# A decoder step on one core: norm sums by one product with ones, prompt rows transposed by VectorE, small work in larger groups

## The chip, the cores and the metric

The kernel runs on one core of a Trainium2 chip. The metric is device time in microseconds (us) of one execution; lower is better. Names of engines in the profile: PE is TensorE (PEld its weight loads), DVE is VectorE, ACT is ScalarE, POOL is GpSimd, SP is the queue that issues most transfers.

## The reference

One layer of a hybrid decoder for 256 prompt tokens and 32 sample tokens (8 sequences of 4), with a model width of 2048, all in float32. Cut to what matters here:

```python
def rms_norm(x, g):
    y = x * lax.rsqrt(jnp.mean(x * x, axis=-1, keepdims=True) + RMS_EPS)
    return y * g

def decoder_layer(x, mk, mv, conv_past, pool_past, pos0, ...):
    h = rms_norm(x, g_mix)
    z = h @ w_in                                   # 2048 -> 11264 columns
    u, v, c, p, gate = jnp.split(z, SPLITS, axis=-1)
    y_a, v_state = chunk_mixer(u, v, ...)          # u * (tril(W_s) LN(v) + b_s), 4 heads
    y_b, conv_state = conv_module(c, conv_past, ...)   # GLU, 31-tap conv, LayerNorm, swish
    y_c, pool_state = pool_mixer(p, pool_past, ...)    # trailing means, linear map
    br = jnp.einsum('bsnc,ncd->bsnd', jnp.stack([y_a, y_b, y_c], axis=2), w_branch)
    merged = jnp.sum(jax.nn.sigmoid(gate) * br, axis=2)
    x = x + merged @ w_out
    x = x + cross_attn(rms_norm(x, g_xattn), mk, mv, w_xq, w_xo)
    hm = rms_norm(x, g_mlp)
    x = x + jnp.square(jax.nn.relu(hm @ w_up)) @ w_down
    return x, v_state, conv_state, pool_state
```

The outputs are the normed x of both groups, the new memory keys and values, and states: the last 30 GLU rows and the last 15 pooling rows of each sequence (new_conv_p and new_pool_p for the prompt), and the normed v rows.

## The kernel before

**Layout.** Activations stand transposed: 128 channels on the partitions, 288 token columns (256 prompt, 32 sample) in the free dimension. A product of 2048 inputs and 512 outputs (proj) runs over 16 k-tiles into four PSUM accumulators of 128x288; there are eight PSUM buffers in all. To keep float32 precision, each operand is split in a high and a low part (w_hi, w_lo; q_hi, q_lo), and every product is three matmuls (L239 to L241).

**Weights.** A chunk of 512x512 (1 MB) is loaded by the SP queue into one of three raw buffers. It is used in two halves of two k-tiles, 24 matmuls each. For each half ScalarE writes w_hi (L172) and VectorE writes w_lo = raw - w_hi (L173). There are three buffers of each, and next_half(i) calls advance(i), which splits half i + 2 (AHEAD = 2); so a half's split is issued two halves before its products.

**Order of other work.** After each half tick() runs. It moves a clock on by one and runs every piece of work that later(n, fn) has put down n steps before, and a few taps of the convolution from a background list. The order of instructions on every engine is the order in which the Python code issues them; each engine executes its own in that order.

**Statistics.** The squares of x (or of the centred convolution) are summed over the 8 or 16 channel tiles into one accumulator of 128x288, acc (square_acc, L334). Still to be summed are the 128 partitions. stats_later does it in three steps, each one tick apart: token_rstd multiplies acc with a column of ones, so that the tokens come to stand on the partitions (L288), scales (L290, L291) and takes the power -0.5 on GpSimd over 128x2 and 32x1 elements (rpow, L283); token_diag makes a diagonal matrix of the result (L300); broadcast_tokens multiplies it with a matrix of ones (L306), which spreads each token's factor over all partitions, and copies it to rb (L308). It is called three times: for the convolution's LayerNorm (used by conv_out, L775, five ticks later), and at the end of residual for the norm before cross attention (used in evac_q, L944) and before the MLP (used in evac_up, L1144). In the last two the factor is used at the first evacuation, since a row's scale can be applied behind the product.

**Prompt states.** rows_out transposes four channel tiles at a time on TensorE (L573), copies them on ScalarE (L574) and issues a transfer from ScalarE's queue; two quarters for the convolution (L589) and two for the pool (L601).

**Others that the change touches.** state_transposed (L457) turns the incoming states, four transposes (L461) and four VectorE copies (L463) at a time, six times. mixing (L705) computes one channel tile of branch A: three products and three VectorE operations, eight times, one tick apart. rows_keep (L1184) transposes four finished channel tiles for the output, nine times.

Of the kernel before, what the change touches and what calls it, by code (L numbers as in the profile page):

```python
# [8 lines left out]
F32 = mybir.dt.float32  # L9
F32R = mybir.dt.float32r  # L10
AF = mybir.ActivationFunctionType
ALU = mybir.AluOpType
# [4 lines left out]
P = 128  # L17
# [4 lines left out]
NT = NP + NS  # L22
# [4 lines left out]
PP = 15  # L27
# [4 lines left out]
TOK = ((0, 128), (128, 128), (256, 32))  # L32
# [6 lines left out]
def decoder_step_kernel(  # L39
# [10 lines left out]
    v_, s_, g_, t_ = nc.vector, nc.scalar, nc.gpsimd, nc.tensor  # L50
# [8 lines left out]
    small = ctx.enter_context(tc.tile_pool(name="small", bufs=2))  # L59
# [7 lines left out]
    def psum():  # L67
        t = ps_pool.tile([P, 512], F32, name="ps", tag="ps")
        return t
# [3 lines left out]
    ones = const.tile([P, P], F32, name="ones")  # L73
    v_.memset(ones, 1.0)
    mhalf = const.tile([P, 3], F32, name="mhalf")
# [21 lines left out]
    def later(n, fn):  # L97
        clock[1] += 1
        pending.append((clock[0] + n, clock[1], fn))
# [143 lines left out]
    def proj(w, nkt, n0, act, evac, bg=0, w_k0=0, last=False):  # L243
        acc = [psum() for _ in range(4)]
        for kc in range(0, nkt, 4):
            if last and kc == nkt - 4:
                hl = [next_half(w, w_k0 + kc + 2 * half, n0) for half in range(2)]
                for j in range(4):
                    for i in range(4):
                        product(acc, act, *hl[i // 2], kc + i, i % 2, j, nkt)  # L250
                    evac(j, acc[j][:, :NT])
                tick()
                return
            for half in range(2):
                hi, lo = next_half(w, w_k0 + kc + 2 * half, n0)
                for i in range(2):
                    kt = kc + 2 * half + i
                    for j in range(4):
                        product(acc, act, hi, lo, kt, i, j, nkt)
                tick(bg)  # L260
        for j in range(4):
            evac(j, acc[j][:, :NT])
# [19 lines left out]
    def rpow(out, ms):  # L282
        g_.tensor_tensor(out, ms, mhalf[:ms.shape[0], :ms.shape[1]], ALU.pow)  # L283

    def token_rstd(acc, n, eps):
        st = psum()
        for i, (t0, tn) in enumerate(TOK):
            t_.matmul(st[:tn, i:i + 1], acc[:, t0:t0 + tn], ones[:, 0:1], start=True, stop=True)  # L288
        ms = small.tile([P, 3], F32, name="ms")
        v_.tensor_scalar(ms[:, 0:2], st[:, 0:2], 1.0 / n, eps, ALU.mult, ALU.add)  # L290
        v_.tensor_scalar(ms[:32, 2:3], st[:32, 2:3], 1.0 / n, eps, ALU.mult, ALU.add)  # L291
        r = small.tile([P, 3], F32, name="r_tok")
        rpow(r[:, 0:2], ms[:, 0:2])
        rpow(r[:32, 2:3], ms[:32, 2:3])
        return r

    def token_diag(r):
        dg = small.tile([P, NT], F32, name="dg", tag="t288", bufs=4)
        for i, (t0, tn) in enumerate(TOK):
            v_.tensor_scalar(dg[:tn, t0:t0 + tn], ident[:tn, :tn], r[:tn, i:i + 1], None, ALU.mult)  # L300
        return dg

    def broadcast_tokens(dg):
        out = psum()
        for t0, tn in TOK:
            t_.matmul(out[:, t0:t0 + tn], ones[:tn, :], dg[:tn, t0:t0 + tn], start=True, stop=True)  # L306
        rb = small.tile([P, NT], F32, name="rb")
        v_.tensor_copy(rb, out[:, :NT])  # L308
        return rb

    def stats_later(acc, n, eps, box, start):
        def s1():
            box["r"] = token_rstd(acc, n, eps)

        def s2():
            box["dg"] = token_diag(box["r"])

        def s3():
            box["rb"] = broadcast_tokens(box["dg"])
        later(start, s1)  # L320
        later(start + 1, s2)
        later(start + 2, s3)

    def t288(name):
        t = small.tile([P, NT], F32, name=name, tag="t288", bufs=4)
        return t
# [22 lines left out]
    for cp in range(4):  # L349
        cs = slice(cp * 512, (cp + 1) * 512)  # L350
# [8 lines left out]
    for vec in (g_mix, g_xattn, g_mlp, g_final, conv_b, ln_c_g, ln_c_b, pool_scale):  # L359
        src = vec[0] if len(vec.shape) == 2 else vec  # L360
        n = src.shape[0] // P
# [72 lines left out]
    gp = glu[:, :8 * 286].rearrange("p (t n) -> p t n", t=8)  # L434
    gs = glu[:, 8 * 286:8 * 286 + 8 * 272].rearrange("p (t b n) -> p t b n", t=8, b=8)
    pf = bp.tile([P, KT * NT], F32, name="pf", tag="m")
    pp = pf[:, :8 * 271].rearrange("p (t n) -> p t n", t=8)
    pq = pf[:, 8 * 271:8 * 271 + 8 * 152].rearrange("p (t b n) -> p t b n", t=8, b=8)
    states = {}
# [17 lines left out]
    def state_transposed(nat, q4, dst, nb):  # L457
        pt = psum()
        for i in range(4):
            t = q4 * 4 + i  # L460
            t_.transpose(pt[:, i * 120:(i + 1) * 120], nat[:120, t * P:(t + 1) * P], ident[:120, :120])  # L461
        for i in range(4):
            v_.tensor_copy(dst(q4 * 4 + i), pt[:, i * 120:(i + 1) * 120].rearrange("p (b r) -> p b r", b=nb))  # L463
# [4 lines left out]
    later(9, conv_weights)  # L468
    for q4 in range(2):
        for hb in range(2):  # L470
            later(10 + 2 * q4 + hb, lambda q4=q4, hb=hb: state_transposed(
                states[f"sc{hb}"], q4, lambda t: gs[:, t, 4 * hb:4 * hb + 4, 0:30], 4))
        later(16 + q4, lambda q4=q4: state_transposed(states["sp"], q4, lambda t: pq[:, t, :, 0:PP], 8))

    wsn = bp.tile([P, 4, P], F32, name="wsn", tag="tmpv")
    wbd = bp.tile([32, 4, 32], F32, name="wbd")
# [38 lines left out]
    def smp(ap):  # L515
        return ap.rearrange("p (b q) -> p b q", q=DQ)
# [51 lines left out]
    def rows_out(src, rows, put):  # L568
        def quarter(q4):
            rt = small.tile([32, 512], F32, name="rt", tag="kn", bufs=3)  # L570
            pt = psum()
            for i in range(4):
                t_.transpose(pt[:rows, i * P:(i + 1) * P], src(q4 * 4 + i), ident)  # L573
            s_.copy(rt[:rows], pt[:rows, :])  # L574
            later(1, lambda: put(rt, slice(q4 * 512, (q4 + 1) * 512)))
        for q4 in range(2):
            later(1 + 2 * q4, lambda q4=q4: quarter(q4))

    def rows_out_sample(src, dst, r0):
        st = small.tile([P, 8, NS], F32, name="stg", tag="t288", bufs=4)  # L580
        for t in range(8):
            s_.copy(smp(st[:, t, :]), src(t))

        def put(rt, cs):
            for b in range(NB):
                nc.sync.dma_start(dst[0, b, r0:r0 + DQ, cs], rt[DQ * b:DQ * b + DQ])
        rows_out(lambda t: st[:, t, :], NS, put)

    rows_out(lambda t: gp[:, t, 256:286], 30, lambda rt, cs: s_.dma_start(new_conv_p[0, 0, :, cs], rt[:30]))  # L589
    later(5, lambda: rows_out_sample(lambda t: gs[:, t, :, 30:34], new_conv_s, 26))  # L590
    later(12, lambda: s_.dma_start(new_conv_s[0, :, 0:26, :], state_conv[0, :, 4:30, :]))
    later(14, lambda: s_.dma_start(new_pool_s[0, :, 0:11, :], state_pool[0, :, 4:15, :]))
# [2 lines left out]
    for half in range(2):  # L595
# [2 lines left out]
            s_.copy(pp[:, t, PP:PP + NP], acc[:, :NP])  # L598
            s_.copy(pq[:, t, :, PP:PP + DQ], smp(acc[:, NP:NT]))
        proj(w_in, KT, 4096 + half * 512, act, evac_p, bg=2)  # L600
    rows_out(lambda t: pp[:, t, 256:271], 15, lambda rt, cs: s_.dma_start(new_pool_p[0, 0, :, cs], rt[:15]))  # L601
    later(5, lambda: rows_out_sample(lambda t: pq[:, t, :, PP:PP + DQ], new_pool_s, 11))

    mix = bp.tile([P, 8, NT], F32, name="mix", tag="u")
# [100 lines left out]
    def mixing(t):  # L705
        h = t // 2
        pt = psum()
        for c in range(2):
            t_.matmul(pt[:, c * P:(c + 1) * P], vn[c][:, t * P:(t + 1) * P], wT[:, h, :], start=True, stop=True)
        t_.matmul(pt[:, NP:NT], vn[2][:32, t * P:(t + 1) * P], wTs[:, h, :], start=True, stop=True)  # L710
        mx = t288("mx")
        v_.tensor_tensor(mx[:, :NP].rearrange("p (c t) -> p c t", c=2), pt[:, :NP].rearrange("p (c t) -> p c t", c=2),
                         bsB[:, h:h + 1, :].to_broadcast([P, 2, P]), ALU.add)
        v_.tensor_tensor(smp(mx[:, NP:NT]), smp(pt[:, NP:NT]), bsB[:, h:h + 1, 0:DQ].to_broadcast([P, NB, DQ]), ALU.add)
        v_.tensor_tensor(u[:, t, :], u[:, t, :], mx, ALU.mult)
    for t in range(8):
        later(1 + t, lambda t=t: mixing(t))


    merged = bp.tile([P, KT, NT], F32, name="merged", tag="m")  # L720
# [176 lines left out]
    act, box = residual(w_out, act, G_XATTN)  # L897
# [122 lines left out]
    hb = {}  # L1020
# [102 lines left out]
    act, box = residual(w_xo, act, G_MLP)  # L1123
# [60 lines left out]
    def rows_keep(j, i):  # L1184
        tn = TOK[i][1]
        s_.copy(y[i, j // 2][:tn, (j % 2) * 512:(j % 2 + 1) * 512], rows(j, i)[:tn, :])

    for j in range(4):
        proj(w_down, KT, j * 512, hid, lambda i, acc, j=j: final(4 * j + i, acc), w_k0=3 * KT, last=j == 3)
        if j < 3:  # L1190
            for i in range(3):
                later(2 + i, lambda j=j, i=i: rows_keep(j, i))

    ms = small.tile([P, 3], F32, name="msf")
    g_.memset(ms, 1.0)
# [7 lines left out]
    r = small.tile([P, 3], F32, name="rf")  # L1203
    rpow(r, ms)
    pts = [rows(3, i) for i in range(3)]
    for i, (t0, tn) in enumerate(TOK):
        rt = r[:tn, i:i + 1]
        dst = y_sample.rearrange("b q d -> (b q) d") if i == 2 else y_prompt[0, t0:t0 + tn, :]
# [37 lines left out]
```

## Time and profile before

| | us |
|---|---|
| median of 3 runs | 2169.7 (2169.19 to 2174.8) |
| profiled execution | 2167.95 |
| its span, first to last instruction | 2166.1 |
| TensorE busy in the span | 2132.5 |
| VectorE | 1284.6 |
| ScalarE | 865.1 |
| GpSimd | 31.3 |

A row of the order of time has start, duration, engine, line of the kernel, operation, output and inputs, shapes and a count (xN: N instructions in a row, merged); in brackets stands idle time before it and what ended it. A row of a group has the count, then busy time in us and the mean of one in ns. Matmuls overlap, so their durations say less than the spacing of their starts. A float32 matmul is recorded as two. A row of windows has the length, then busy time and count of PE, PEld, DVE, ACT and POOL, then the granted TensorE clock, the DMA share and GB/s.

### The profile page before, as it was taken

The numbers are of one execution on the slowest core, as the hardware profiler recorded it, in microseconds if no ns is written. First come the engines' busy times: TensorE is split into PE (matmuls) and PEld (weight loads), VectorE is DVE, ScalarE is ACT, GpSimd is POOL, SyncE is SP. The second block draws the span as 40 slices with busy tenths as digits, with TensorE's granted clock in tenths as the row PEclk, the third lists the DMA queues.
The fourth block names the chain that finished last, engine by engine and source line by source line (L and its number), as shares of the span: only waits on it lengthen the run. The fifth ranks groups of instructions, "written<-read, shape, count | busy, mean of one in ns | idle before, by whom it ended". The sixth has DMA issues, their size and how long they took to land.

```text
span 2166.1 us, 36855 instructions
## 1 busy us (share of the span) xinstructions
PE 2132.5 (98%) x15559; PEld 2060.2 (95%) x15559; DVE 1284.6 (59%) x1955; ACT 865.1 (40%) x1189; POOL 31.3 (1%) x93
## 2 busy tenths in 40 slices
PE   8999999999999999998899999999999999999998
PEld 7999999999999999995677899999999999999997
DVE  7767877677565657555555646554454445545554
ACT  5444433343345434352334534333333333333343
POOL 1000000000000000001000000000000000000000
PEclk9999999999999999999899999999999999999999
DMA  7546444544545577769998554545554555455542
GB/s 248 192 150 212 159 156 156 168 164 158 174 157 174 201 216 206 203 195 233 284 335 278 178 167 157 174 158 174 157 174 157 174 158 173 159 172 160 172 156 103
DMA packets 223417, 397.50 MB, mean 184 GB/s; under 512 B 9402, under 2 KB 47930, under 8 KB 222843
## 3 DMA queue, kind: packets, MB, share of 16 engines
q1 hardware_dynamic: 218117, 384.37, 55.8%
q10 hardware_dynamic: 4878, 10.72, 1.4%
q8 instruction: 122, 2.00, 0.4%
q14 instruction: 44, 0.36, 0.1%
q0 software_dynamic: 256, 0.05, 0.0%
HBM read 383.51 MB, written 12.80 MB: 183 GB/s over the span
## 4 chain that ended last, share of the span: by engine, by line
PE 56%; issue 38%; DMA 4%; DVE 1%; SPq 1%; ACT 0%; POOL 0%; ACTq 0%; POOLq 0%; DVEq 0%
PE ps L241 15%; PE ps L239 15%; PE ps L240 15%; PE ps L274 2%; PE ps L275 2%; PE ps L276 2%; DMA kv<-in_cache_mem_k_dram 1%; DMA raw<-in_w_xk_dram 1%; PE ps L1003 1%; SPq L852 0%; DMA raw<-in_w_in_dram 0%; DVE w_lo L173 0%; PE ps L647 0%; ACT w_hi L172 0%; DMA k_scr<-kn 0%
## 5 line engine op out<-in xcount | busy, mean ns | idle before, releaser
L173 DVE TENSOR_TENSOR w_lo<-raw,w_hi 128x1024 fp32r<-128x1024 f32 (+1 forms) x673 | 785.5, 1172 | 818.3 <-ACT w_hi L172 815.4
L172 ACT CAST w_hi<-raw 128x1024 fp32r<-128x1024 f32 (+1 forms) x673 | 673.4, 1007 | 1156.6 <-PE ps L240 964.0
L239 PE MATMUL ps<-q_hi,w_hi 128*128 128x288 f32 x3200 | 946.9, 296 | 1.7 <-ACT w_hi L172 1.2
L241 PE MATMUL ps<-q_hi,w_lo 128*128 128x288 f32 x3200 | 943.7, 295 | 1.2 <-DVE w_lo L173 1.2
L240 PE MATMUL ps<-q_lo,w_hi 128*128 128x288 f32 x3200 | 943.4, 295 | 0.7 <-DVE q_lo L200 0.7
L239 PEld LDWEIGHTS ps<-q_hi,w_hi 128*128 128x128 f32 x3200 | 601.0, 188 | 3.1 <-ACT w_hi L172 1.4
L240 PEld LDWEIGHTS ps<-q_lo,w_hi 128*128 128x128 f32 x3200 | 601.2, 188 | 1.5 <-DVE q_lo L200 0.9
L241 PEld LDWEIGHTS ps<-q_hi,w_lo 128*128 128x128 f32 x3200 | 600.6, 188 | 1.7 <-DVE w_lo L173 1.6
L241 PE MATMUL ps<-h_hi,w_lo 128*128 128x288 f32 x1024 | 302.2, 295 | 0.0
L239 PE MATMUL ps<-h_hi,w_hi 128*128 128x288 f32 x1024 | 301.9, 295 | 0.0
L240 PE MATMUL ps<-h_lo,w_hi 128*128 128x288 f32 x1024 | 301.5, 294 | 0.0
L239 PEld LDWEIGHTS ps<-h_hi,w_hi 128*128 128x128 f32 x1024 | 192.1, 188 | 0.0
L240 PEld LDWEIGHTS ps<-h_lo,w_hi 128*128 128x128 f32 x1024 | 192.1, 188 | 0.0
L241 PEld LDWEIGHTS ps<-h_hi,w_lo 128*128 128x128 f32 x1024 | 192.1, 188 | 0.0
L274 PE MATMUL ps<-w_hi,q_hi 128*128 128x512 f32 x256 | 102.7, 406 | 11.4 <-ACT w_hi L172 11.4
L241 PE MATMUL ps<-y_hi,w_lo 128*128 128x288 f32 x384 | 113.3, 295 | 0.0
L240 PE MATMUL ps<-y_lo,w_hi 128*128 128x288 f32 x384 | 113.1, 294 | 0.0
L239 PE MATMUL ps<-y_hi,w_hi 128*128 128x288 f32 x384 | 113.0, 294 | 0.0
L527 DVE SCALAR_TENSOR_TENSOR cv<-glu,cwT,cv 128x256 f32<-128x256 f32 x240 | 105.9, 478 | 0.0
L275 PE MATMUL ps<-w_lo,q_hi 128*128 128x512 f32 x256 | 103.0, 402 | 1.7 <-DVE w_lo L173 1.7
L276 PE MATMUL ps<-w_hi,q_lo 128*128 128x512 f32 x256 | 101.5, 397 | 0.0
L274 PEld LDWEIGHTS ps<-w_hi,q_hi 128*128 128x128 f32 x256 | 48.6, 192 | 29.3 <-ACT w_hi L172 16.9
(301 smaller groups left out, 1277.1 us busy)
## 6 DMA issues: line engine op xcount, KB each, us to landing
raw<-in_w_in_dram SPq DMA_DIRECT2D x87, 1024.0 KB
raw<-in_w_up_dram SPq DMA_DIRECT2D x64, 1024.0 KB
raw<-in_w_down_dram SPq DMA_DIRECT2D x64, 1024.0 KB
raw<-in_w_branch_dram SPq DMA_DIRECT2D x24, 1024.0 KB
raw<-in_w_out_dram SPq DMA_DIRECT2D x16, 1024.0 KB
kv<-in_cache_mem_k_dram SPq DMA_DIRECT2D x128, 128.0 KB
raw<-in_w_xq_dram SPq DMA_DIRECT2D x16, 1024.0 KB
raw<-in_w_xk_dram SPq DMA_DIRECT2D x16, 1024.0 KB
```

What stands on the lines that cost most here:

```text
L172: latest["hi"] = s_.copy(dh, src)
L173: latest["lo"] = v_.tensor_tensor(dl, src, dh.bitcast(F32), ALU.subtract)
L239: t_.matmul(o, wh, act.hi(kt), start=kt == 0, stop=False)
L240: t_.matmul(o, wh, act.lo(kt), start=False, stop=False)
L241: t_.matmul(o, wl, act.hi(kt), start=False, stop=kt == nkt - 1)
L274: t_.matmul(acc[c], mh, hi[:, i, :], start=kt == 0, stop=False)
L275: t_.matmul(acc[c], mh, lo[:, i, :], start=False, stop=False)
L276: t_.matmul(acc[c], ml, hi[:, i, :], start=False, stop=kt == KT - 1)
L527: v_.scalar_tensor_tensor(o, i, wk, o, ALU.mult, ALU.add)
L1003: t_.matmul(sbox["osc"][32 * h:32 * h + 32, :], pTm[:, c, h, :], vraw[4 * b + 2 * c + h // 2][:, (h % 2) * 512:(h % 2 + 1) * 512], start=b ...
```

## The change

1. stats_later becomes one step. One product of the whole matrix of ones with acc gives every partition the sums of all 288 tokens; VectorE scales them from PSUM to SBUF, and GpSimd takes the power over 128x288 elements, straight into rb. token_rstd goes; token_diag and broadcast_tokens remain for the first norm alone.
2. The prompt's state rows are no longer transposed by TensorE: rows_out_prompt has VectorE transpose blocks of 32x32 in one instruction of 128x256, and four transfers on ScalarE's queue write runs of 32 values each.
3. State transposes come in three groups instead of six, mixing in two groups of four, and the three transposes of rows_keep in one tick.

```diff
-    def token_rstd(acc, n, eps):
-        st = psum()
-        for i, (t0, tn) in enumerate(TOK):
-            t_.matmul(st[:tn, i:i + 1], acc[:, t0:t0 + tn], ones[:, 0:1], start=True, stop=True)
-        ...
-        return r
 ...
     def stats_later(acc, n, eps, box, start):
         def s1():
-            box["r"] = token_rstd(acc, n, eps)
-
-        def s2():
-            box["dg"] = token_diag(box["r"])
-
-        def s3():
-            box["rb"] = broadcast_tokens(box["dg"])
+            st = psum()
+            t_.matmul(st[:, :NT], ones, acc, start=True, stop=True)
+            ms = t288("msq")
+            v_.tensor_scalar(ms, st[:, :NT], 1.0 / n, eps, ALU.mult, ALU.add)
+            rb = small.tile([P, NT], F32, name="rb")
+            g_.tensor_tensor(rb, ms, mhalf[:, 0:1].to_broadcast([P, NT]), ALU.pow)
+            box["rb"] = rb
         later(start, s1)
-        later(start + 1, s2)
-        later(start + 2, s3)
 ...
-            later(10 + 2 * q4 + hb, lambda q4=q4, hb=hb: state_transposed(
+            later(10 + 2 * q4, lambda q4=q4, hb=hb: state_transposed(
                 states[f"sc{hb}"], q4, lambda t: gs[:, t, 4 * hb:4 * hb + 4, 0:30], 4))
-        later(16 + q4, lambda q4=q4: state_transposed(states["sp"], q4, ...))
+        later(16, lambda q4=q4: state_transposed(states["sp"], q4, ...))
 ...
-    rows_out(lambda t: gp[:, t, 256:286], 30, lambda rt, cs: s_.dma_start(new_conv_p[0, 0, :, cs], rt[:30]))
+    def rows_out_prompt(last, dst, rows):
+        rt = small.tile([P, 8, 32], F32, name="rt", tag="t288", bufs=4)
+        v_.transpose(rt, last)
+
+        def put():
+            for a in range(4):
+                s_.dma_start(dst.rearrange("n (t a r) -> a n t r", t=8, a=4)[a], rt[32 * a + 32 - rows:32 * a + 32])
+        later(1, put)
+    later(1, lambda: rows_out_prompt(gp[:, :, 254:286], new_conv_p[0, 0], 30))
 ...
-    rows_out(lambda t: pp[:, t, 256:271], 15, lambda rt, cs: s_.dma_start(new_pool_p[0, 0, :, cs], rt[:15]))
+    later(1, lambda: rows_out_prompt(pp[:, :, 239:271], new_pool_p[0, 0], 15))
 ...
     for t in range(8):
-        later(1 + t, lambda t=t: mixing(t))
+        later(2 + t // 4 * 4, lambda t=t: mixing(t))
 ...
             for i in range(3):
-                later(2 + i, lambda j=j, i=i: rows_keep(j, i))
+                later(3, lambda j=j, i=i: rows_keep(j, i))
```

More of the change, by code (lines that the diff above doesn't have):

```diff
@@ L283, in rpow @@
         g_.tensor_tensor(out, ms, mhalf[:ms.shape[0], :ms.shape[1]], ALU.pow)
-    def token_rstd(acc, n, eps):
-        st = psum()
-        for i, (t0, tn) in enumerate(TOK):
[L288 to L294, printed above, removed]
-        return r
     def token_diag(r):
@@ L470, in decoder_step_kernel @@
         for hb in range(2):
-            later(10 + 2 * q4 + hb, lambda q4=q4, hb=hb: state_transposed(
+            later(10 + 2 * q4, lambda q4=q4, hb=hb: state_transposed(
                 states[f"sc{hb}"], q4, lambda t: gs[:, t, 4 * hb:4 * hb + 4, 0:30], 4))
-        later(16 + q4, lambda q4=q4: state_transposed(states["sp"], q4, lambda t: pq[:, t, :, 0:PP], 8))
+        later(16, lambda q4=q4: state_transposed(states["sp"], q4, lambda t: pq[:, t, :, 0:PP], 8))
     wsn = bp.tile([P, 4, P], F32, name="wsn", tag="tmpv")
```

## The prediction

> **What bounds the kernel now.** I read the page first (span and busy shares), then the order of time on TensorE around each place the change touches, then GpSimd's instructions one by one with VectorE's beside them.
>
> ```profile
> span 2166.1 us, 36855 instructions
> PE 2132.5 (98%) x15559; PEld 2060.2 (95%) x15559; DVE 1284.6 (59%) x1955; ACT 865.1 (40%) x1189; POOL 31.3 (1%) x93
> ```
>
> TensorE is the bound, busy for 98% of the span; VectorE has 41% to spare and GpSimd does next to nothing. So an instruction taken off TensorE's stream is time saved, whatever VectorE or ScalarE save is worth nothing, and what makes VectorE late for its low weight halves (w_lo) is time lost. How late it may be follows from the code: a half's split is issued two halves ahead of its products.
>
> **Statistics, TensorE's side.** stats_later is called three times: the convolution's LayerNorm (at 631 us), the RMS norms before cross attention (869) and before the MLP (1336). Here is TensorE's order of time at the first: three stretches, the last of the conv_mean product, which has the form that the change introduces (ones times a 128x288 accumulator, recorded as two passes).
>
> ```profile
> 631.36 0.30 PE L241 MATMUL ps<-q_hi,w_lo 128*128 128x288 f32 x1
> 631.49 0.65 PE L288 MATMUL ps<-ones,acc 128*128 128x1 f32 x6
> 632.31 0.30 PE L240 MATMUL ps<-q_lo,w_hi 128*128 128x288 f32 x1
> ...
> 638.41 0.29 PE L241 MATMUL ps<-q_hi,w_lo 128*128 128x288 f32 x1
> 638.54 0.94 PE L306 MATMUL ps<-dg,ones 128*128 128x128 f32 x6
> 639.40 0.40 PE L239 MATMUL ps<-q_hi,w_hi 128*128 128x288 f32 x1
> 639.64 0.29 PE L240 MATMUL ps<-q_lo,w_hi 128*128 128x288 f32 x1
> ...
> 618.15 0.29 PE L241 MATMUL ps<-q_hi,w_lo 128*128 128x288 f32 x1
> 618.28 0.65 PE L762 MATMUL ps<-acc,ones 128*128 128x288 f32 x2
> 618.90 0.29 PE L240 MATMUL ps<-q_lo,w_hi 128*128 128x288 f32 x1
> ```
>
> Products start every 0.13 us: from 632.31 to 638.41 are 46 starts, so one takes 0.1326 and a half of 24 takes 3.18. From the L241 before a group to the L240 behind it undisturbed products would take two starts, 0.265. So L288 costs 632.31 - 631.36 - 0.265 = 0.69, L306 costs 639.64 - 638.41 - 0.265 = 0.97, and the new product will cost what L762 does, 618.90 - 618.15 - 0.265 = 0.49. One use saves 1.17, three save 3.5 us. The VectorE work saved (diagonals, copy) is off the path.
>
> **Prompt rows.** Sixteen transposes go, in four groups of four. Beside one of these stands a group of eight in one place, for the parts that are only merged:
>
> ```profile
> 131.02 0.29 PE L241 MATMUL ps<-q_hi,w_lo 128*128 128x288 f32 x1
> 131.15 0.60 PE L573 MATMUL ps<-ident,glu 128*30 128x128 f32 x4
> 131.72 0.29 PE L240 MATMUL ps<-q_lo,w_hi 128*128 128x288 f32 x1
> ...
> 244.05 0.29 PE L241 MATMUL ps<-q_hi,w_lo 128*128 128x288 f32 x1
> 244.18 1.03 PE L679 MATMUL ps<-ident,vgt 128*128 128x128 f32 x8
> 245.19 0.30 PE L240 MATMUL ps<-q_lo,w_hi 128*128 128x288 f32 x1
> ```
>
> Four cost 131.72 - 131.02 - 0.265 = 0.44, so the four groups give 1.75 us. In their place VectorE transposes 128x256 twice (under half a microsecond each, as the 288-column operations below) and ScalarE's queue issues eight DMAs instead of four, with runs of 128 bytes. ScalarE loses four copies, has 60% idle, and nobody waits for these outputs. If the issues held up its next w_hi, the two halves of lookahead cover it. I take nothing.
>
> **Larger groups.** Eight transposes cost 245.19 - 244.05 - 0.265 = 0.88, twice 0.44: a group has no price of its own, so merging mixing (eight places to two), state transposes (six to three) and final transposes (nine to three) gains nothing. At most it saves the 0.1 by which the first product behind a group is spaced wider, 15 times, 1.5 us. Against it: half of the states' copies move one step earlier, in the first 70 us, where VectorE has most to do; four copies there are about 1.2 us (by the 0.3 to 0.45 us of other operations of that width). I take a loss of 0.5, an estimate, with bounds of -1.5 and +1.2 for all merges. Four mixings hold the four PSUM banks that the gate's product leaves; each is evacuated while the next is computed.
>
> **The power, GpSimd's side.** This decides. Before, pow ran over a token column per 128 tokens, two or three elements a partition. Now one instruction takes it over 128x288, because the sums are already spread over the partitions. The trace has it alone with three, two and one columns (the last from the groups in the stretch 871 to 874.3 us):
>
> ```profile
> 2155.64 0.85 POOL L283 TENSOR_TENSOR rf<-msf,mhalf 128x3 f32<-128x3 f32 x1 [815.63 <-DVE msf L1202]
> 976.37 0.70 POOL L283 TENSOR_TENSOR r_mem<-ms,mhalf 128x2 f32<-128x2 f32 x1 [1.76 <-DVE ms L927]
> L283 POOL TENSOR_TENSOR r_tok<-ms,mhalf 32x1 f32<-32x1 f32 x1 | 0.6, 569 | 0.0
> ```
>
> 0.57, 0.70, 0.85: each column adds 0.13 to 0.15 us. No longer pow is in the trace, so I bound it: below by a price that stops growing (under 1 us), above by 0.16 a column (46.5 us). Full-width forms give 0.15, and I take it: 0.70 + 286 x 0.15 = 43.6 us.
>
> The Trainium skill, GPSIMD Engine Reference, section 3.1, gives about 2.6 cycles an element for a two-input operation at 1.2 GHz; an estimate by it is 288 x 2.6 / 1.2 = 620 ns for the columns, and the sum would be the third rival's. The trace does not agree for pow: 130 to 150 ns a column, not 2.2.
>
> **Who waits for it.** GpSimd and VectorE exclude each other, the trace shows, at least one way:
>
> ```profile
> 1131.63 0.21 POOL L987 COPY pTm<-psT 128x32 f32<-128x32 f32 x1
> 1150.87 0.90 POOL L987 COPY pTm<-psT 128x32 f32<-128x32 f32 x1
> 1150.47 1.22 DVE L173 TENSOR_TENSOR w_lo<-raw,w_hi 128x1024 fp32r<-128x1024 f32 x1
> ...
> 632.42 1.86 POOL L283 TENSOR_TENSOR r_tok<-ms,mhalf 128x2 f32<-128x2 f32 x2 [367.11 <-DVE ms L291]
> 632.64 1.22 DVE L173 TENSOR_TENSOR w_lo<-raw,w_hi 128x1024 fp32r<-128x1024 f32 x1 [0.24 <-ACT w_hi L172]
> ```
>
> A copy of 0.21 took 0.90 when a w_lo (two operands from SBUF) was running, and ended 0.08 behind it. A whole VectorE instruction holds the operands' way, and GpSimd waits it out. The simplest reading is a lock for whoever comes first, and then w_lo waits out a long pow. The last pair is the only row the other way: a w_lo that started 0.22 us into a pow was not lengthened. But two columns may have been read by then; 288 columns are read over most of 43 us. So I hold the lock the likelier.
>
> The Trainium skill, SBUF — State Buffer, section "Who interferes with whom", says so: a VectorE instruction with two SBUF inputs contends with a GpSimd one that reads SBUF, and whoever issues first blocks the other for its whole length. By it the time is the forecast below, without it that of the first rival. The 0.90 agrees for one direction; no run here shows a long GpSimd instruction.
>
> **The stalls.** The rows that place them:
>
> ```profile
> 636.54 1.22 DVE L173 TENSOR_TENSOR w_lo<-raw,w_hi 128x1024 fp32r<-128x1024 f32 x1 [1.99 <-ACT w_hi L172]
> 648.15 0.45 DVE L775 TENSOR_TENSOR tn__7059<-cv,rb 128x288 f32<-128x288 f32 x1
> 871.25 1.27 DVE L173 TENSOR_TENSOR w_lo<-raw,w_hi 128x512 fp32r<-128x512 f32 x2
> 880.08 0.40 PE L239 MATMUL ps<-q_hi,w_hi 128*128 128x288 f32 x1
> 891.91 1.66 DVE L944 TENSOR_TENSOR q<-ps,rb 128x288 f32<-128x288 f32 x4 [0.17 <-PE ps L241]
> 1337.70 1.20 DVE L173 TENSOR_TENSOR w_lo<-raw,w_hi 128x1024 fp32r<-128x1024 f32 x1
> 1343.77 0.40 PE L239 MATMUL ps<-q_hi,w_hi 128*128 128x288 f32 x1
> 1358.88 0.45 DVE L1144 TENSOR_TENSOR z<-ps,rb 128x288 f32<-128x288 f32 x1
> ```
>
> In each place VectorE scales the sums (0.45, as other 288-column operations), and a w_lo follows at once, which pow waits out; 43.6 us later the lock is free, and the next w_lo runs. With TensorE's stream 1.2 us earlier than now:
> - Convolution: that w_lo ends at 633.9, pow at 677.5. The next w_lo (now at 636.54) ends at 678.7. Its products are due a half after 639.40, less 1.2: 641.4. Stall 37.3.
> - Cross attention: w_lo ends at 0.35 behind 872.5 because of the longer scaling, 872.9; pow ends at 916.5, the first piece of the next w_lo at 917.1. Due at 880.08 less 1.35 (its first group of products waited, so 0.2 more is saved): 878.7. Stall 38.4.
> - MLP: w_lo ends at 1339.2 (1337.70 + 1.20, and 0.3 for the longer scaling), pow at 1382.8, the next w_lo at 1384.0; due a half after 1343.77, less 1.2: 1345.8. Stall 38.2.
>
> Behind VectorE stand the loads (a raw buffer is free only after w_lo); they wait too, but then three chunks are already there. ScalarE's w_hi is ready. On GpSimd nothing is queued behind pow that is due in these stretches. After such a pause TensorE's clock drops:
>
> ```profile
> 1020.00:1030.00 10.00, 2.23 (x16) 0.83 (x8) 1.94 (x2) 1.96 (x2) 0.76 (x2) 0.83 1.13 250
> 1030.00:1040.00 10.00, 7.90 (x28) 5.53 (x28) 4.05 (x5) 1.40 (x3) 0.00 (x0) 0.83 1.17 251
> ```
>
> In these windows (the granted clock is the third column from the end) it idles for most of the first ten microseconds, and in the next the clock is 0.83: 1.7 us lost. Three times, 5.1.
>
> **Sum.** 37.3 + 38.4 + 38.2 + 5.1 - 3.5 - 1.75 + 0.5 = +114.3. The profiled execution took 2167.95 us (1.9 around its span); it lies 0.1% below the median of 2169.7. Forecast 2282. With 0.13 a column pow takes 37.9 and the time is 2265, with 0.16 it is 2291: its own range is 2262 to 2300.
>
> **Rivals.**
> 1. No lock in that direction: VectorE runs on until it needs the result, at L775, L944 and L1144. Then the stall is the end of pow less the consumer's present start, plus 1.2, less about 3.7 (two halves of lookahead, 6.4, less 2.7 for the consumer and a w_lo): 26.9, 22.1 and 21.4, together 70.4, so 2239; if the w_lo in between hold pow up by 1.2 us each, some five a place, up to 2257. For it: the w_lo at 632.64.
> 2. A column gets cheaper in a long instruction, but not cheap: 0.03 to 0.12 us, pow 9 to 35 us. With the lock a place stalls by about pow less 5.5: 2180 to 2255. For it: only that three columns are few.
> 3. Pow over 288 columns takes 5.5 us or less, and all is hidden: 2167.95 - 5.25 + 0.5 = 2163, 0.2% faster, not slower. It decides at 0.02 us a column; the three rows above speak against it, that they may be start-up cost for it. With the merges at their best this becomes 2161, which is just the 0.3% below the profiled execution.
>
> **Chances.** Forecast 0.50, rival 1 0.22, rival 2 0.10, rival 3 0.14; 0.04 for more than 2310 or another cause. Leaving out rival 3 and the ends, the range is 2180 to 2310. A change of 0.3% (6.5 us) is about what this measurement can tell. Faster 0.05 and same 0.11 come from rival 3 and the low end of rival 2; slower 0.84.
>
> **What would show it.** In the changed kernel's GpSimd rows the pow 128x288 at about 43 us, three times; TensorE idle after each, with w_lo as what it waits for, and w_lo either standing for 40 us right after the sums (forecast) or only at L775, L944 and L1144 (rival 1). L288, L306 and the prompt's L573 gone; the new product at 0.49, groups of eight transposes at 0.88. The forecast is wrong if pow stays under 6 us: the one figure it hangs on is a slope from three columns.

## The result, and the profile after

| | before | after |
|---|---|---|
| median of 4 runs each, on the same chip | 2171.35 (2169.19 to 2174.8) | 2248.89 (2242.52 to 2251.57) |
| profiled execution | 2167.95 | 2248.87 |
| its span | 2166.1 | 2247.1 |

The ratio is 1.0358, with a 95% interval of 1.0346 to 1.0371: 3.6% slower. The size lies in the range given, but well below the 2282 forecast. It is the first rival, not the forecast, that came about. Of all executions reported below one, of the kernel with the grouping alone, took 10592.86 us and is left out of that kernel's median and interval.

From the page of the changed kernel:

```profile
span 2247.1 us, 36753 instructions
PE 2137.9 (95%) x15513; PEld 2064.0 (92%) x15513; DVE 1282.5 (57%) x1942; ACT 862.4 (38%) x1185; POOL 166.2 (7%) x90
PE   8999999999968999599799999599999999999998
POOL 1000000000070000801000001600000000000000
PEclk9999999999989999799899999799999999999999
L306 POOL TENSOR_TENSOR rb<-msq,mhalf 128x288 f32<-128x288 f32 x3 | 141.6, 47196 | 637.0 <-DVE msq L304 637.0
```

TensorE's busy time has hardly moved, while the span grew by 81 us: the loss is waiting. GpSimd went from 31.3 to 166.2 us; three instructions of 47.2 us, 141.6 together, are more than the whole rise. In the 40 slices GpSimd's three busy places stand where TensorE's row has its new dips; the granted clock dips with them.

VectorE's waits for GpSimd, by line (total, times, longest):

```profile
DVE tn__7025 L769 <- POOL rb L306: 32.9, 1, 32.9
DVE q L938 <- POOL rb L306: 28.3, 1, 28.3
DVE z L1138 <- POOL rb L306: 27.5, 1, 27.5
```

These are the three consumers, which were L775, L944 and L1144 before. VectorE didn't stop ahead of them; here are GpSimd's and then VectorE's order of time around the first power:

```profile
630.43 47.25 POOL L306 TENSOR_TENSOR rb<-msq,mhalf 128x288 f32<-128x288 f32 x1 [367.41 <-DVE msq L304]
```

```profile
630.36 1.23 DVE L173 TENSOR_TENSOR w_lo<-raw,w_hi 128x1024 fp32r<-128x1024 f32 x1
634.05 1.23 DVE L173 TENSOR_TENSOR w_lo<-raw,w_hi 128x1024 fp32r<-128x1024 f32 x1 [2.47 <-ACT w_hi L172]
...
643.56 1.22 DVE L173 TENSOR_TENSOR w_lo<-raw,w_hi 128x1024 fp32r<-128x1024 f32 x1 [1.96 <-ACT w_hi L172]
677.71 0.46 DVE L769 TENSOR_TENSOR tn__7025<-cv,rb 128x288 f32<-128x288 f32 x1 [32.93 <-POOL rb L306]
...
679.80 1.23 DVE L173 TENSOR_TENSOR w_lo<-raw,w_hi 128x1024 fp32r<-128x1024 f32 x1 [0.47 <-ACT w_hi L172]
```

Inside a running power of 47 us four w_lo start and take their normal 1.22 to 1.23 us. VectorE then stands at L769 for 32.9 us until the power ends at 677.68, and the next w_lo, queued behind it, starts only at 679.80. ScalarE is caught in the same way:

```profile
678.21 0.63 ACT L771 ACTIVATE sgm<-tn__7025,gvec 128x288 f32<-128x288 f32 x1 [34.68 <-DVE tn__7025 L769]
678.74 1.03 ACT L172 CAST w_hi<-raw 128x1024 fp32r<-128x1024 f32 x1
```

Its sigmoid needs VectorE's output, and the w_hi behind the sigmoid waits with it. TensorE's order of time: the new product, and then the pause that follows:

```profile
629.08 0.29 PE L241 MATMUL ps<-q_hi,w_lo 128*128 128x288 f32 x1
629.21 0.65 PE L302 MATMUL ps<-acc,ones 128*128 128x288 f32 x2
...
629.82 0.29 PE L240 MATMUL ps<-q_lo,w_hi 128*128 128x288 f32 x1
...
651.82 0.29 PE L241 MATMUL ps<-q_hi,w_lo 128*128 128x288 f32 x1
679.82 0.61 PE L239 MATMUL ps<-q_hi,w_hi 128*128 128x288 f32 x1 [27.71 <-ACT w_hi L172]
...
681.08 0.61 PE L241 MATMUL ps<-q_hi,w_lo 128*128 128x288 f32 x1 [0.41 <-DVE w_lo L173]
681.49 0.44 PE L239 MATMUL ps<-q_hi,w_hi 128*128 128x288 f32 x1
...
684.57 0.30 PE L240 MATMUL ps<-q_lo,w_hi 128*128 128x288 f32 x1
...
948.15 0.61 PE L241 MATMUL ps<-q_hi,w_lo 128*128 128x288 f32 x1 [22.56 <-DVE w_lo L173]
```

The halves split ahead keep TensorE going until 651.82, though VectorE's last w_lo ended at 644.78. From start to start the pause is 28.00 us here, 22.85 in cross attention (925.30 to 948.15) and 22.91 in the MLP (1422.19 to 1445.10). Afterwards products start every 0.24 us and not every 0.13 until about 684.5. The same in two windows of 10 us (the third column from the end is the granted clock):

```profile
660.00:670.00 10.00, 0.00 (x0) 0.00 (x0) 0.00 (x0) 0.00 (x0) 10.00 (x1) 0.50 0.00 0
...
680.00:690.00 10.00, 9.59 (x57) 9.24 (x58) 8.65 (x16) 6.16 (x12) 0.00 (x0) 0.77 0.33 107
```

From 660 to 670 nothing but GpSimd runs, not even the loads.

Where the 81.0 us of the span went:

| part | us |
|---|---|
| three pauses, beyond the 0.13 from one product to the next (27.87 + 22.72 + 22.78) | +73.4 |
| three restarts (products late against a spacing of 0.13: 2.6 + 2.8 + 2.3) | +7.7 |
| stage of the cached keys, from its first product to the first of the cached values (102.3 to 108.2) | +5.9 |
| TensorE's savings: 2.28 before 629.21 (the same product group started at 631.49 before), and 1.17 at each statistic | -5.8 |

The sum is +81.2.

### The profile page after: what moved, and what is told of

The parts are those of the page before. It is cut to its first block, busy times and chain, and to the rows that moved or that the text cites. A ratio compares the mean times of both kernels' runs of the same rounds, so it can differ in the third digit from the quotient of the medians.

```text
span 2247.1 us, 36753 instructions
## 1 busy us (share of the span) xinstructions
PE 2137.9 (95%) x15513; PEld 2064.0 (92%) x15513; DVE 1282.5 (57%) x1942; ACT 862.4 (38%) x1185; POOL 166.2 (7%) x90
## 4 chain that ended last, share of the span: by engine, by line
issue 52%; PE 36%; POOL 6%; DMA 3%; DVE 1%; ACT 0%; SPq 0%; ACTq 0%; POOLq 0%; DVEq 0%
PE ps L241 9%; PE ps L240 9%; PE ps L239 9%; POOL rb L306 6%; PE ps L274 2%; PE ps L275 2%; PE ps L276 2%; DMA raw<-in_w_xk_dram 1%; DMA kv<-in_cache_mem_k_dram 1%; PE ps L997 1%; DMA raw<-in_w_in_dram 0%; PE ps L641 0%; DVE w_lo L173 0%; DMA out_dram<-kn 0%; ACT w_hi L172 0%
## 5 line engine op out<-in xcount | busy, mean ns | idle before, releaser
L306 POOL TENSOR_TENSOR rb<-msq,mhalf 128x288 f32<-128x288 f32 x3 | 141.6, 47196 | 637.0 <-DVE msq L304 637.0
```

The lines of the kernel that those rows point to most:

```text
L306: g_.tensor_tensor(rb, ms, mhalf[:, 0:1].to_broadcast([P, NT]), ALU.pow)
```

## The experiments

The theory (A in the expectations): a power over 128x288 takes 47 us, VectorE waits for it only where it uses the result, and that is the whole loss. The rivals put part of the loss on the other edits, on the grouping, or on what a long GpSimd instruction takes from VectorE merely by running.

**The old statistics in the changed kernel, and the new ones alone in the kernel before.**

e1_stats_old is the changed kernel with token_rstd and the three steps of stats_later as before. e2_stats_only is the kernel before with stats_later's one step as in the change, and nothing else.

> The changed kernel with the old three-step statistics; prompt rows and groups stay changed. Theory A (the whole loss is the three long pows): TensorE saves only the prompt's transposes, 1.75 us, so 2169.6 against 2171.35, ratio 0.999. Theory B (other parts share in the loss, such as the 5.9 us that the stage of cross attention's keys is longer in the changed kernel): 2175 or more, ratio above 1.002.

> The kernel before with the new statistics alone. Theory A: the changed kernel's time plus the 1.75 us of the prompt's transposes, 2250.6, ratio 1.0365. Theory B: the loss is smaller by what the other parts cost, 2245 or less, ratio 1.034 or less.

Measured: with the old statistics 2167.45, ratio 0.9991 (0.9980 to 1.0001); with the new statistics alone 2247.13, ratio 1.0363 (1.0349 to 1.0376). In the second the powers take 47.25, 47.20 and 47.13 us, and VectorE's three waits are 32.9, 28.3 and 27.5, as in the changed kernel. So the loss is the statistics', and all of it as far as these intervals tell (some 3 us to either side).

**The same value without GpSimd.** ScalarE takes the root and VectorE the reciprocal:

```diff
-            g_.tensor_tensor(rb, ms, mhalf[:, 0:1].to_broadcast([P, NT]), ALU.pow)
+            sq = t288("rt_")
+            s_.activation(sq, ms, AF.Sqrt)
+            v_.reciprocal(rb, sq)
```

> The changed kernel with the power taken by ScalarE (square root) and VectorE (reciprocal) in place of GpSimd, all else as changed. Theory A: no long instruction is left, the factor is there after about 3 us, and what remains is TensorE's saving, 3.5 + 1.75: 2166, ratio 0.9976. Rival: ScalarE must load a table for the root and again for what follows (1.28 us each in the profile before), which comes on top of w_hi and makes TensorE wait: 2168 to 2174, ratio 0.999 to 1.001.

Measured: 2167.18, ratio 0.9987 (0.9978 to 0.9996). The 81 us are gone with the one instruction. What stands in its place, on VectorE and then on ScalarE:

```profile
632.51 1.95 DVE L308 RECIPROCAL rb<-rt__6871 128x288 f32<-128x288 f32 x1 [0.62 <-ACT rt__6871 L307]
```

```profile
630.73 1.28 ACT L307 ACT_TABLE_LOAD   x1
632.03 0.45 ACT L307 ACTIVATE rt__6871<-msq 128x288 f32<-128x288 f32 x1
632.49 1.28 ACT L721 ACT_TABLE_LOAD   x1
```

The root needs a table load of 1.28 us, the next function another, and the reciprocal 1.95 us, four times what VectorE's other 288-column operations take. All of it fits in the slack, and TensorE does not pause. The gain over before is between what the two theories had; the last experiments come back to that.

**The price, and whether running costs anything.** Six more powers that nobody waits for, three widths in each of two quarters of the MLP, put into the kernel before; in the second quarter VectorE gets extra two-operand work as well:

```diff
+    v_.memset(pin, 2.0)
 ...
+        for n in (288, 144, 72):
+            g_.tensor_tensor(pout[:, :n], pin[:, :n], mhalf[:, 0:1].to_broadcast([P, n]), ALU.pow)
 ...
+        for n in range(2):
 ...
+            v_.tensor_tensor(bz, gpair[0], gpair[1], ALU.add)
 ...
+                for n in range(30):
+                    later(1 + n, busy)
```

> The kernel before with pows of 128x288, 128x144 and 128x72 added for which nobody waits, once in the first quarter's w_down stage and once in the second's; in the second VectorE also gets two additions of 128x512, both operands from SBUF, after every half, so that it runs two-operand instructions for some 80% of the time instead of 40%. Theory A (a price per column, no interference): 47, 24 and 12 us in both stages, and the time stays within 0.3% of before. Theory C (the two engines hold each other up): pow's bare price is about 41 us and each two-operand VectorE instruction that it meets adds its own length: 60 to 70 us in the first stage, above 90 in the second. If a running pow held VectorE up (the lock of the prediction), the time would grow by some 35 us for each of the long ones, 2240 or more.

Measured: 2235.85, ratio 1.0305 (1.0292 to 1.0319), which no theory had. GpSimd's order of time, and VectorE's:

```profile
1239.83 163.99 POOL L1142 TENSOR_TENSOR pout<-pin,mhalf 128x288 f32<-128x288 f32 x6 [69.55 <-DVE pin L1138]
1403.79 1.24 POOL L283 TENSOR_TENSOR r_tok<-ms,mhalf 128x2 f32<-128x2 f32 x2
```

```profile
1337.77 0.14 DVE L291 TENSOR_SCALAR ms<-ps 32x1 f32<-32x1 f32 x1
...
1404.52 0.78 DVE L300 TENSOR_SCALAR dg<-ident,r_tok 128x128 f32<-128x128 f32 x3 [65.48 <-POOL r_tok L283]
```

All six ran in one go from 1239.83, long before the place where the code has them; their input had been written just before, at 1239.39. The MLP's own two powers, 1.24 us together, came behind them, and VectorE waited 65.5 us for them. So the statement in the description above, that the order on every engine is the one in which the code issues the instructions, was written too broadly: it did not hold for these GpSimd instructions, whose input was early. Whether the building of the program or the chip moved them ahead, the runs don't show. The run says again what a short result behind a long GpSimd instruction costs, but not what it was meant to.

Repeated with the input written late, by VectorE, from the last tile of the quarter:

```diff
-    v_.memset(pin, 2.0)
 ...
+        v_.tensor_scalar(pin, late, 0.0, 2.0, ALU.mult, ALU.add)
```

> The kernel of e4, with the added pows reading a tile that VectorE writes after the up products of each quarter, so that they can't go ahead of the statistics on GpSimd's queue, as they did in e4. Theory A (a price per column, no interference either way): 46.5, 23.3 and 12.0 us, as in e4, in the first quarter's w_down stage (VectorE in two-operand instructions for some 45% of the time) and in the second's (some 85%); time within 0.3% of before. Theory C (each two-operand instruction that a pow meets adds its length): 60 to 80 us for the long one in the first, above 90 in the second. Lock theory (a running pow holds VectorE's two-operand instructions up): 2240 or more.

Measured: 2171.42, ratio 1.0007 (0.9996 to 1.0017). Some 170 us of powers that nobody waits for cost nothing that can be measured. GpSimd's groups in the window 1446 to 1528 us, then in 1640 to 1730:

```profile
L1142 POOL TENSOR_TENSOR pout<-pin,mhalf 128x288 f32<-128x288 f32 x1 | 46.2, 46233 | 103.0 <-PE ps L241 103.0
L1142 POOL TENSOR_TENSOR pout<-pin,mhalf 128x144 f32<-128x144 f32 x1 | 23.3, 23297 | 0.1
L1142 POOL TENSOR_TENSOR pout<-pin,mhalf 128x72 f32<-128x72 f32 x1 | 11.8, 11839 | 0.1
```

```profile
L1142 POOL TENSOR_TENSOR pout<-pin,mhalf 128x288 f32<-128x288 f32 x1 | 53.0, 53017 | 121.6 <-DVE pin L1140 121.6
```

From 72 to 144 columns the price rises by 11.46 us, from 144 to 288 by 22.94: 0.159 us a column, with no start-up to speak of. The 53.0 has its reason in VectorE's order of time at its start, 1649.23:

```profile
1649.07 1.22 DVE L173 TENSOR_TENSOR w_lo<-raw,w_hi 128x1024 fp32r<-128x1024 f32 x1
1650.20 1.28 DVE L1147 TENSOR_TENSOR bz<-gp,gp 128x512 f32<-128x512 f32 x2
...
1654.88 1.28 DVE L1147 TENSOR_TENSOR bz<-gp,gp 128x512 f32<-128x512 f32 x2
1656.66 1.23 DVE L173 TENSOR_TENSOR w_lo<-raw,w_hi 128x1024 fp32r<-128x1024 f32 x1 [0.49 <-ACT w_hi L172]
```

VectorE runs two-operand instructions without a gap until 1656.16 (1654.88 + 1.28). From there to the power's end at 1702.25 are 46.1 us. The power waited until VectorE's first gap, and then ran its normal time although VectorE was busy for 37.9 of those 46.1 us. The same holds in the changed kernel: the first power started 0.07 behind the start of a w_lo that ended at 631.59, and from there to 677.68 are 46.1 us.

The power behind it, of 144 columns, shows that a gap is not needed, and that VectorE can be held up as well. Here it is with the pair of additions beside its start; below it stand the second long power of the run before this one (e4) and two VectorE operations beside its start:

```profile
1702.33 23.79 POOL L1142 TENSOR_TENSOR pout<-pin,mhalf 128x144 f32<-128x144 f32 x1
1702.28 1.52 DVE L1147 TENSOR_TENSOR bz<-gp,gp 128x512 f32<-128x512 f32 x2
...
1321.74 46.79 POOL L1142 TENSOR_TENSOR pout<-pin,mhalf 128x288 f32<-128x288 f32 x1
1322.38 1.35 DVE L200 SCALAR_TENSOR_TENSOR q_lo<-xT,gvec,q_hi 128x288 fp32r<-128x288 f32 x2
```

The power took 23.79 us, not 23.30, and the pair 1.52, not 1.28: the power came in between two additions, and the second waited for it, some 0.2 us. In e4 the pair took 1.35 and not 0.94. In the traces of all these kernels seven VectorE instructions with two tensors as inputs are more than 0.05 us longer than the median of their kind. All seven start within 1.5 us of the start of a power of 72 columns or more, and they are 0.07 to 0.41 us longer; none is in the rest of a power. So a power and a VectorE instruction do hold each other up, but the power holds VectorE up only for some tenths of a microsecond at its start, as it would if it read its whole input there. Why one power waited over several VectorE instructions and another over one is open.

**Half a power.** The power over 144 columns; the other half of rb is a copy of the scaled sums, so those columns are not normalised rightly:

```diff
-            g_.tensor_tensor(rb, ms, mhalf[:, 0:1].to_broadcast([P, NT]), ALU.pow)
+            g_.tensor_tensor(rb[:, :NT // 2], ms[:, :NT // 2], mhalf[:, 0:1].to_broadcast([P, NT // 2]), ALU.pow)
+            v_.tensor_copy(rb[:, NT // 2:], ms[:, NT // 2:])
```

> The changed kernel with pow over 144 of the 288 columns; for the other columns VectorE copies the sums (the power is left out there). Theory A (0.162 us a column): pow takes 23.8 us, 23.4 less. The pauses of TensorE, 28.0, 22.9 and 22.9 us, shrink to 4.6, 0 and 0, and two of three slow restarts (2.6 us each) go: 2248.9 - 23.4 - 22.8 - 22.8 - 5 = 2175, ratio 1.002. A price that lies mostly in a fixed part of the instruction would leave it near 2249; the lock of the prediction (w_lo waits for pow's end) would leave three pauses of some 18 us, 2225.

Measured: 2175.29, ratio 1.0025 (1.0014 to 1.0036). VectorE's waits:

```profile
DVE tn__7026 L770 <- POOL rb L306: 10.0, 1, 10.0
DVE q L939 <- POOL rb L306: 5.5, 1, 5.5
DVE z L1139 <- POOL rb L306: 4.7, 1, 4.7
```

The power is 24.3 to 24.4 us, so half of it takes 22.8 us off each wait. Only the first still makes TensorE pause, for 5.1 us: the lookahead hides the waits of 5.5 and 4.7 wholly, and of the 10.0 about half.

**The consumer later.** The convolution's outputs eleven steps later:

```diff
-        later(12 + t, lambda t=t: conv_out(t))
+        later(23 + t, lambda t=t: conv_out(t))
```

> The changed kernel with the convolution's normalisation (conv_out) 23 to 30 steps after its start instead of 12 to 19, still ahead of its use. Theory A (only the consumer waits): VectorE reaches the factor some 35 us later than now, when pow is done; the first pause and its restart go, 28 + 2.6 us: 2218, ratio 1.0217. Rival (the lock, or w_lo hindered by a running pow): the first pause stays, 2245 to 2249.

Measured: 2215.35, ratio 1.0207 (1.0186 to 1.0228). The first power still takes 47.25 us; when the consumer comes, at 679.96, it has ended 2 us before, VectorE doesn't wait, and the first pause is gone. The waits of 28.3 and 27.5 in the other two places remain. So what costs is the wait at the consumer, not the power's running; here too TensorE goes on beside the running power. In the other two places there is nothing to put between: the first evacuation needs the factor.

**The other parts alone**, in the kernel before: e7_prompt_only takes rows_out_prompt, e8_merge_only the three changed calls of later.

> The kernel before with the prompt's rows transposed by VectorE alone. Theory A: 1.75 us off TensorE's stream, 2169.6, ratio 0.9992. Rival: the eight transfers with runs of 128 bytes hold up weight loads or ScalarE: no gain or a loss, ratio 1.000 to 1.003.

> The kernel before with the larger groups alone (states, mixing, final transposes). Theory A: a group has no price of its own, ratio 1.000 (0.9993 to 1.0006). Rival: each change between kinds of products costs TensorE some 0.1 us or more, 15 fewer give 1.5 us or more: ratio 0.9993 or less.

Measured: prompt rows 2166.34, ratio 0.9989 (0.9979 to 0.9999); grouping 2170.53, ratio 1.0002 (0.9990 to 1.0014). The first agrees with the 1.75 us worked out, though its interval reaches from 0.2 to 4.6 us; the second agrees with no price for a group, and its interval holds the rival's 1.5 us too.

**A version that beats both, and what the grouping may cost in the key stage.** The kernel before, with the one-product statistics by root and reciprocal and with the prompt rows, without the grouping (e10); the kernel before once more (e11, one execution); and e3's kernel once more (e12).

> The kernel before with the statistics by one product, the power by ScalarE's square root and VectorE's reciprocal, and the prompt's rows by VectorE; no larger groups. Theory A: 5.25 us off TensorE's stream, 2164.7, ratio 0.9976. Rival D (the stage of cross attention's keys, which waits on transfers, gives the gain back; it took 108.0 us in e3 against 102.3 before): 2167 to 2170, ratio 0.9985 to 0.9995.

> The kernel before once more, for a second profile of the stage of cross attention's keys, from its first product with cached keys to the first with cached values: 102.3 us in the first profile. If that stage differs from run to run by itself (rival E), it lies anywhere from 101 to 109 here; if its length belongs to the kernel (rival D), 102 to 103.

> e3 once more beside e10 on one chip, and a second profile of the same stage: 108.0 us in e3's. Rival D: 107 to 109 again, ratio 0.9985 to 0.999. Rival E: anywhere from 101 to 109, ratio as e10's.

Measured: e10 2164.81, ratio 0.9970 (0.9959 to 0.9981); e11 2163.48 in its one run; e12 2165.39, ratio 0.9980 (0.9971 to 0.9990). The best is e10, at what the sum of the savings (3.5 + 1.75 of 2170 is 0.9976) leads one to expect. Its interval overlaps with e12's, so that the grouping costs anything there is not shown by the times.

Of the two repeats, e11's key stage of 98.6 us (below) lies outside what either rival said; e12's of 107.7 fits rival D, but its ratio of 0.9980 lies outside D's.

The length of the key stage, from the first product with the cached keys to the first with the cached values, is 102.3 us before and 108.2 after, by these lines of the two traces (first and last start stand behind the durations; before, then after):

```profile
L874 PE MATMUL ps<-kT,qm x256: 376/379/403, 976.8 to 1058.7; 128*32 128x256 f32 x128
L1003 PE MATMUL ps<-kv,pTm x128: 592/592/617, 1079.1 to 1209.9; 128*32 128x512 f32 x128
```

```profile
L868 PE MATMUL ps<-kT,qm x256: 379/379/403, 1028.3 to 1114.7; 128*32 128x256 f32 x128
L997 PE MATMUL ps<-kv,pTm x128: 592/592/617, 1136.5 to 1267.2; 128*32 128x512 f32 x128
```

| kernel, one profile each | key stage, us |
|---|---|
| before; the same again (e11) | 102.3; 98.6 |
| old statistics with grouping (e1; grouping alone, e8) | 104.4; 101.6 |
| new statistics without grouping (e2, e10) | 102.8; 102.0 |
| prompt rows alone (e7); added powers (e4, e9) | 103.6; 102.5, 104.4 |
| new statistics and grouping (after, e3, e12, e6, e5) | 108.2, 108.0, 107.7, 108.9, 105.5 |

Only kernels that have both parts reach 105.5 and more, whatever takes the power; all five have the prompt rows as well. The stage moves by some 6 us in the others too, so that five profiles are few. In every one of these traces it moves 26.6 to 26.9 MB, at 271 GB/s in the shortest and 246 to 248 in the four longest, and in the four of them where the waits were read (before, after, e10, e12) ScalarE's w_hi waits 51 to 57 us for loaded chunks: the stage's length goes with the rate of the transfers. What sets that rate, and whether the two parts have a share in it, stays open. e12's profiled execution took 2168.69, 3.3 us above its median, so its stage may be longer than that kernel's usual one.

## Why the prediction was right or wrong

**Right: that the power decides, and that the other edits do little.** The new product costs 629.82 - 629.08 - 0.265 = 0.48 (0.49 said), the prompt rows agree with 1.75 (e7), their two VectorE transposes take 0.43 and 0.44 us. Groups have no price of their own: in TensorE's order of time of the changed kernel, twelve final transposes

```profile
2162.80 0.29 PE L241 MATMUL ps<-h_hi,w_lo 128*128 128x288 f32 x1
2162.93 1.47 PE L1175 MATMUL ps<-ident,xT 128*128 128x128 f32 x12
...
2164.37 0.29 PE L240 MATMUL ps<-h_lo,w_hi 128*128 128x288 f32 x1
```

cost 2164.37 - 2162.80 - 0.265 = 1.31, three times the 0.44 of four.

**Right but for the size: the slope of the power.** A line through one, two and three columns held up to 288. The column costs 0.159, not 0.15; from the end of the w_lo ahead of it the power takes 46.1 where 43.6 was said. The upper bound, 46.5, was the better value.

**Wrong: the lock.** The step that failed is "288 columns are read over most of 43 us", for which no row stood, and with it "So I hold the lock the likelier" and the three stalls of 37.3, 38.4 and 38.2. A w_lo does not wait for a running power: it took 1.22 to 1.23 us inside it, four times over in the first place alone, and what a power holds up it holds up by 0.07 to 0.41 us, at its start. The copy of 0.90 us, on which the step rested, showed the other direction, and that one is right, but only for the start of the GpSimd instruction (53.0 against 46.2 us). The row that spoke against a long lock, the w_lo of 632.64 that ran undisturbed inside a power of two columns, was at hand. The prediction granted that two columns may have been read by then, which fits what the runs showed, but took reading to last as long as the instruction. The Trainium skill, SBUF — State Buffer, section "Who interferes with whom", has the first to issue block the other for its whole length. By the runs here that holds for a power behind a VectorE instruction; a VectorE instruction behind a power was held for at most 0.41 of its 47 us.

That the time lies in the range owes nothing to this mechanism: the range reached down over the rivals, and the one that came about had a chance of 0.22, less than half of the forecast's 0.50.

**What stood in the lock's place** is rival 1, term by term. It had waits of 30.6, 25.8 and 25.1 less 3.7 of lookahead. Measured were 32.9, 28.3 and 27.5, each 2.3 to 2.5 more, as the power's 2.5 makes it, less 4.7 to 5.6 (27.87, 22.72 and 22.78 remain): lookahead hides more than was worked out. Together +3.0. The prediction's "ScalarE's w_hi is ready" did not hold in two of the three places: in the convolution w_hi stood behind the sigmoid, and in the MLP behind ScalarE's cast of the first output, which waited 29.8 us for VectorE; TensorE's pause ended with w_hi in both.

**Mis-sized: the restart,** 1.7 said, 2.3 to 2.8 measured, +2.6 for the three together. The window it was taken from lies behind a pause of 7.4 us; that the length of the pause matters is not shown, for the pauses of 22.85 and 22.91 us gave 2.8 and 2.3. The Trainium skill, TensorE: Matmul & The Clock Gate, Part 1, has the clock at one half until about 3.4 us of sustained work. The first restart agrees (products 0.24 apart from 681.08 to 684.4), and the waits of the first products come on top; in the second the wide spacing lasted longer, 5.9 us (948.15 to 954.08).

**Not foreseen: the key stage,** +5.9 in the profiled execution, of which the cause is open. From rival 1: 2239 + 3.0 + 2.6 + 5.9, less 1.0 because the savings are 5.8 and not the net 4.75, is 2249.5, against 2248.9.

## What to carry to other kernels

An operation that is nothing on three columns can be the longest instruction of the kernel on 288, and a slope from the small forms in the trace predicts it: so take the power while the sums are still few to a partition and spread the result, or take it another way: root and reciprocal over all 288 columns (e10) gave the lowest ratio of these kernels, 0.9970. A long instruction on an idle engine costs nothing as long as nobody waits for it or for what stands behind it on its engine (as in e4), and its price is the wait at the first consumer less the lookahead; so look for what is queued behind that consumer on its engine, and for whether there is room to put the consumer later. Where a row of the trace shows one direction of a conflict, the other has to be read from a row of its own, and how long an instruction holds what both need is not its duration.

## What the runs showed of the hardware that was not expected

- GpSimd's power costs 0.159 us a column of 128 partitions, evenly from 72 to 288 columns, and 46.1 us for 288.
- A power that starts while VectorE runs two-operand instructions waits for VectorE (1.1 us behind one w_lo; 6.9 us behind a row of instructions without a gap; 0.5 us where it came in between two additions). The two long ones then took 46.1 us, with VectorE nearly idle and with VectorE 82% busy.
- Seven two-operand instructions of VectorE that began within 1.5 us of a power's start were 0.07 to 0.41 us longer than usual; in the rest of a power none was longer by more than 0.05 us (w_lo 1.22 to 1.23 us). That the power reads its whole input in these first tenths is the simplest reading, and is not shown directly.
- VectorE's reciprocal of 128x288 takes 1.95 us, other operations of that shape 0.45.
- GpSimd instructions without a late input ran ahead of those that the code issues before them, and a result of 1.24 us then came 65 us late; whether the chip or the building of the program put them there is not shown.
